# The MLP of the last two token blocks as seven half-size products per layer

## The chip, the cores and the metric

The kernel runs on one core of a Trainium2 chip. The metric is the device time in microseconds (us) of one execution. The engines are PE (TensorE, matrix products; PEld is its load of the stationary operand), DVE (VectorE), ACT (ScalarE), POOL (GpSimd) and SP (SyncE, which here issues the DMA transfers). SBUF holds the working tiles, PSUM the results of products in banks of 128 x 512 float32, and DRAM the inputs, outputs and scratch.

## The reference

One layer over 2048 tokens of 1024 channels, behind 16 learned meta tokens. A normed input is projected; two scans run over the sequence in chunks (a gated delta rule and a gated linear attention, four heads each); their gated outputs, 1024 columns wide, go through one output projection and are added to the input; then an MLP with squared ReLU, 1024 to 4096 to 1024, and a final norm.

```python
mix = jnp.concatenate([o_dn, o_gla], axis=-1).astype(x.dtype)
x = x + mix @ w_out
h2 = rmsnorm(x, norm2_g)
x = x + jnp.square(jax.nn.relu(h2 @ w_up)) @ w_down
...
return rmsnorm(h, final_norm_g)[:, CHUNK:]
```

The delta rule's state goes from chunk to chunk, so the mixed output of a block of tokens is complete only when the scan has passed its last chunk.

## The kernel before

The tokens are in four blocks of 512, the chunks in sixteen of 128, scanned in pairs. The program runs: input projection of blocks 0 and 1 (`phase_a`), scan of the meta tokens and of chunks 0 to 3, input projection of blocks 2 and 3, scan of chunks 4 to 11, `phase_c(0)`, scan of chunks 12 to 15, `phase_c(1)`, and `phase_c(2)` for blocks 2 and 3 together. `phase_c` is output projection and MLP. Most instructions of the program stand in the order that a scheduler gave them, so work of neighbouring calls is mixed: parts of the scan stand among the MLP's products, and block 1's output projection stands among the scan of chunk 11 to 13. Each engine runs its own list in order.

Channels lie on the partitions, tokens along the free dimension. Every product is made of three (L117 to L119): each float32 operand is split into a hi part, rounded to the PE's format, and a lo part, the difference, and hi x hi, lo x hi and hi x lo are summed in PSUM. A weight chunk of 128 x 1024 is loaded by SP into one of three raw buffers (L97), cast to hi by ACT (L101) and its lo part made by DVE (L102), in two buffers each. Activations are split the same way (L109 and L110; with a scale L112 and L113).

Per block the output projection has 192 products of 512 columns, the up layer 768 and the down layer 768. In `phase_c` the scan's output is read back from `mix_d` (L858), the projection is added to the input in `acc` (L896), `h2` is split from it, and the squares are summed in `tot` (ACT L882, POOL L883). The norm ahead of the MLP is made up for behind it (`norm`, L909 to L913), so the up layer starts without it. For each of eight groups g: four banks of the up layer, ReLU and square (L961, L962), split, and the group's share of the down layer, added to `acc` on DVE (L974). `finish` is the final norm: column sums of `tot` by PE (`pf`, L925), the power by POOL (L930), broadcast by PE (`pfb`, L939), eight scaled rows by DVE (L950) and the output. For block 0 and block 1 it is kept in `after` and run in the next scan pair or after `phase_c(1)`.

For blocks 2 and 3 each weight chunk serves both blocks, and the last of the eight groups goes by tokens, block 3 in two halves of 256, so that little is left after the last product.

The scan's mixed outputs are transposed (L812) and stored (L815) in `flush_mix`. A pair's triangular matrices are inverted on DVE in rows (L564, L570), and both U and the inverse V pass through DRAM (SP, L555, L560, L572, L578).

Of the kernel before, what the change touches and what calls it, by code (L numbers as in the profile page):

```python
# [8 lines left out]
F32 = mybir.dt.float32  # L9
# [7 lines left out]
D = 1024  # L17
SEQ = 2048
NMETA = 16
EPS = 1e-6  # L20
# [10 lines left out]
# log1p(e) = e * P(e) on [0, 1] to float32 accuracy.  # L31
# [10 lines left out]
def hybrid_kernel(ctx: ExitStack, tc: tile.TileContext, I: dict, out: bass.AP):  # L42
# [7 lines left out]
    wk = ctx.enter_context(tc.tile_pool(name="work", bufs=2))  # L50
# [70 lines left out]
    # ------------------------------------------------------------------ scratch in DRAM  # L121
# [6 lines left out]
    mix_d = [dp.tile([128, 8, TB], F32, name=f"mix_d{b}") for b in range(NB)]  # L128

    # ------------------------------------------------------------------ scan constants and state  # L130
# [21 lines left out]
    # ------------------------------------------------------------------ phase A: input projection  # L152
    def phase_a(b, kc, late=None):
# [3 lines left out]
        def log1p(e, p, shape, tag):  # L157
            """log(1 + e) for e in [0, 1], in a new tile."""
# [9 lines left out]
        def normless(k):  # L168
            """hi and lo parts of the transposed input times the norm gain, without 1 / rms."""
# [54 lines left out]
        def step(between):  # L224
            """the next part of each job; those that need a PSUM bank wait for the end of a group."""
# [84 lines left out]
        def gla_decay(sm, p, nt, dst, done=None):  # L310
            """cumulated log-sigmoid gates (before the division by the normalizer) into dst[j] of [128, nt * p]."""
# [29 lines left out]
        def gate_piece(y, t, c0, n):  # L341
            """columns c0..c0+n of the gates of token tile t: twice their silu."""
# [9 lines left out]
        def decays():  # L352
            """sets up the work on the decays; it runs in small parts among the groups."""
# [95 lines left out]
    # ------------------------------------------------------------------ phase B: the two scans  # L449
# [11 lines left out]
    def dn_pre(c):  # L461
        """everything of a chunk's delta rule that does not need the state; c None: the meta tokens."""
# [54 lines left out]
        # decay matrix, grams  # L517
# [24 lines left out]
    def dn_inverse(rs, vts):  # L542
        """V = (I - strict upper part of U)^-1 per chunk and head, into vts."""
# [44 lines left out]
            # 32 -> 64: the off-diagonal blocks of the two 64-blocks  # L588
# [21 lines left out]
            # 64 -> 128  # L610
# [10 lines left out]
    def post(po, scale, gate, mix):  # L621
        """per-head RMS norm of po * scale, times the gate."""
# [177 lines left out]
    after = []  # work on a block of tokens that is left for a later place  # L800
# [38 lines left out]

    # ------------------------------------------------------------------ phase C: output projection, MLP  # L840
    def phase_c(b0, pools, bank, kc, tail=None):
# [3 lines left out]
        nh = len(pools)  # L845
        # acc[i][k]: the residual stream of block i, channels 128 k..
        acc, xp = [], []
        for i, q in enumerate(pools):
            pairs = [k4("acc", q).rearrange("p (k t) -> p k t", k=2) for _ in range(4)]
            for j, t in enumerate(pairs):  # L850
                nc.sync.dma_start(out=t, in_=I["xT"][b0 + i, 2 * j : 2 * j + 2].rearrange("k p t -> p k t"))
            xp.append(pairs)
            acc.append([pairs[k // 2][:, k % 2, :] for k in range(NK)])
        mx = [[] for _ in pools]
        for i, q in enumerate(pools):
            for k in range(NK):
                m = tail.tile([128, 512], F32, name="mixk", tag="mixk", bufs=4) if tail else t512("mixk")
                nc.sync.dma_start(out=m, in_=mix_d[b0 + i][:, k, :])  # L858
                o = act("mx", q)
                split(m, *o, gain[:, k // 4 : k // 4 + 1])  # L860
                mx[i].append(o)

        def products(chunks, mov):
            """banks[j][i]: 128 output channels j of block i."""
            banks = [[bank("pc") for _ in pools] for _ in range(4)]
            last = len(chunks) - 1
            for c, src in enumerate(chunks):
                _, wh, wl = wchunk(src, 512)
                for j in range(4):
                    js = slice(j * 128, (j + 1) * 128)  # L870
# [264 lines left out]
```

## Time and profile before

| | us |
|---|---|
| median of three runs | 2658.26 |
| the runs | 2654.13 to 2667.26 |
| span of the profiled execution | 2658.3 |
| mean duration of a product of 128 x 512 in the MLP (they overlap) | 0.39 |
| lo part of a weight chunk, 128 x 1024, on DVE (mean) | 1.26 |
| hi part of a weight chunk on ACT (mean) | 1.05 |

The profile's page says for each engine how long it was busy. Its views list windows of time with busy times, the granted clock of PE and the DMA rate; groups of instructions by line; and the timeline, where a bracket behind a row gives the idle time of the engine before it and what ended that. L12 is line 12 of the kernel.

### The profile page before, as it was taken

What the parts mean: (1) busy time and instruction counts of PE and PEld (TensorE: products, weight loads), DVE (VectorE), ACT (ScalarE), POOL (GpSimd) and SP (SyncE); (2) the same over time, 40 slices, a digit from 0 to 9 for tenths busy, and PEclk for the clock granted to TensorE, in tenths of its full rate; (3) what the DMA queues carried; (4) which work ended last, traced back from release to release, by engine and by line L of the source; (5) the groups of instructions that cost most, each with busy time, mean ns of one, the idle gap of its engine ahead of it and who ended that gap; (6) DMA issues with size and microseconds to landing.
All of it is one profiled execution on the core that took longest, in us unless ns stands there. A gap on an engine that the chain in (4) does not pass through costs nothing.

```text
span 2658.3 us, 35430 instructions
## 1 busy us (share of the span) xinstructions
PE 2569.2 (97%) x13426; PEld 2127.1 (80%) x13426; DVE 1625.0 (61%) x3122; ACT 905.4 (34%) x1850; POOL 475.8 (18%) x385
## 2 busy tenths in 40 slices
PE   8999999999899999999998999999999999999998
PEld 6788688789678778888786888888888888888887
DVE  4777866985984875857679567555453343233335
ACT  4344345345334433334353243333321122112212
POOL 2123123223222321102044020101230000000003
PEclk9999999999999999999999999999999999999999
DMA  5264455355346323334363343253211111111111
GB/s 180 102 214 146 139 152 182 111 187 174 126 154 201 103 89 124 104 106 127 115 208 94 100 121 105 86 175 108 98 48 48 48 48 48 48 48 48 48 48 64
DMA packets 187122, 297.30 MB, mean 112 GB/s; under 512 B 33584, under 2 KB 116104, under 8 KB 186952
## 3 DMA queue, kind: packets, MB, share of 16 engines
q1 hardware_dynamic: 186952, 295.05, 35.5%
q8 instruction: 105, 1.72, 0.3%
q14 instruction: 65, 0.53, 0.1%
HBM read 244.62 MB, written 50.37 MB: 111 GB/s over the span
## 4 chain that ended last, share of the span: by engine, by line
PE 63%; DVE 9%; issue 2%; DMA 2%; POOL 1%; ACT 0%; SPq 0%; POOLq 0%; DVEq 0%; ACTq 0%
PE pc L119 18%; PE pc L118 18%; PE pc L117 18%; PE pa L117 2%; PE pa L118 2%; PE pa L119 2%; DVE wlo L102 1%; DVE inv_t L564 1%; DVE inv_v L570 1%; PE pks L650 1%; DVE l1p L163 0%; PE po L661 0%; PE pu L664 0%; PE po L660 0%; PE py L654 0%
## 5 line engine op out<-in xcount | busy, mean ns | idle before, releaser
L101 ACT CAST whi<-wraw 128x1024 fp32r<-128x1024 f32 (+1 forms) x344 | 346.9, 1009 | 1067.8 <-PE pc L118 813.0
L102 DVE TENSOR_TENSOR wlo<-wraw,whi 128x1024 fp32r<-128x1024 f32 (+1 forms) x280 | 344.8, 1232 | 576.3 <-ACT whi L101 575.2
L118 PE MATMUL pc<-avl,whi 128*128 128x512 f32 (+1 forms) x1056 | 413.1, 391 | 2.5 <-DVE avl L110 2.4
L117 PE MATMUL pc<-avh,whi 128*128 128x512 f32 (+1 forms) x1056 | 397.4, 392 | 12.2 <-DVE acc L974 12.0
L119 PE MATMUL pc<-avh,wlo 128*128 128x512 f32 (+1 forms) x1056 | 406.7, 389 | 0.0
L117 PE MATMUL pc<-h2h,whi 128*128 128x512 f32 x1024 | 402.0, 393 | 2.8 <-DVE acc L896 2.8
L118 PE MATMUL pc<-h2l,whi 128*128 128x512 f32 x1024 | 402.7, 393 | 0.0
L119 PE MATMUL pc<-h2h,wlo 128*128 128x512 f32 x1024 | 399.1, 396 | 1.1 <-DVE wlo L102 1.1
L117 PEld LDWEIGHTS pc<-avh,whi 128*128 128x128 f32 x1056 | 199.6, 189 | 57.3 <-issue 13.3
L118 PEld LDWEIGHTS pc<-avl,whi 128*128 128x128 f32 x1056 | 199.4, 189 | 47.1 <-DVE avl L110 4.8
L119 PEld LDWEIGHTS pc<-avh,wlo 128*128 128x128 f32 x1056 | 199.4, 189 | 42.8
L883 POOL TENSOR_TENSOR tot<-tot,sqk 128x512 f32<-128x512 f32 (+1 forms) x63 | 84.5, 1347 | 824.3 <-ACT sqk L882 822.5
L117 PEld LDWEIGHTS pc<-h2h,whi 128*128 128x128 f32 x1024 | 192.5, 188 | 46.1 <-DVE acc L896 4.1
L119 PEld LDWEIGHTS pc<-h2h,wlo 128*128 128x128 f32 x1024 | 192.3, 188 | 44.4 <-DVE wlo L102 1.9
L118 PEld LDWEIGHTS pc<-h2l,whi 128*128 128x128 f32 x1024 | 192.4, 188 | 42.6
L974 DVE TENSOR_TENSOR acc<-acc,pc 128x512 f32<-128x512 f32 x240 | 162.2, 685 | 104.3 <-PE pc L119 101.9
L102 POOL TENSOR_TENSOR wlo<-wraw,whi 128x780 fp32r<-128x780 f32 (+1 forms) x64 | 142.9, 2233 | 433.2 <-ACT whi L101 345.0
L117 PE MATMUL pa<-hh,whi 128*128 128x512 f32 x512 | 206.6, 405 | 4.2 <-ACT whi L101 2.3
L118 PE MATMUL pa<-hl,whi 128*128 128x512 f32 x512 | 202.7, 396 | 0.0
L119 PE MATMUL pa<-hh,wlo 128*128 128x512 f32 x512 | 188.8, 400 | 2.0 <-DVE wlo L102 1.2
L117 PE MATMUL pa<-whi,hh 128*128 128x390 f32 x512 | 167.8, 357 | 13.8 <-ACT hh L112 11.2
L118 PE MATMUL pa<-wlo,hh 128*128 128x390 f32 x512 | 180.4, 354 | 0.1
(274 smaller groups left out, 4079.7 us busy)
## 6 DMA issues: line engine op xcount, KB each, us to landing
wraw<-in_wup_dram SPq DMA_DIRECT2D x96, 512.0 KB, 3.6
wraw<-in_wdn_dram SPq DMA_DIRECT2D x96, 512.0 KB, 3.6
wraw<-in_wch_dram SPq DMA_DIRECT2D x64, 512.0 KB, 3.7
wraw<-in_wtk_dram SPq DMA_DIRECT2D x64, 390.0 KB, 3.9
qkv_d<-cy SPq DMA_DIRECT2D x48, 256.0 KB, 2.3
kqv<-qkv_d SPq DMA_DIRECT2D x16, 768.0 KB, 5.3
wraw<-in_wo_dram SPq DMA_DIRECT2D x24, 512.0 KB, 3.6
xk<-in_xT_dram SPq DMA_DIRECT2D x32, 256.0 KB, 4.2
```

The costliest lines, as they stand in the source:

```text
L101: A.copy(out=hi[:, :, 0:n], in_=raw[:, :, 0:n])
L102: eng.tensor_tensor(out=lo[:, :, 0:n], in0=raw[:, :, 0:n], in1=hi[:, :, 0:n].bitcast(F32), op=ALU.subtract)
L117: T.matmul(o, lhsT=ah, rhs=bh, start=first, stop=False)
L118: T.matmul(o, lhsT=ah, rhs=bl, start=False, stop=False)
L119: T.matmul(o, lhsT=al, rhs=bh, start=False, stop=last)
L564: V.tensor_tensor(out=t, in0=vv[:, 0:c, c : c + 1].broadcast_to([L, c, n]), in1=vv[:, c : c + 1, c + 1 : w].broadcast_to([L, c, n]), op=AL ...
L570: V.tensor_tensor(out=vv[:, 0:c, c + 1 : w], in0=vv[:, 0:c, c + 1 : w], in1=t, op=ALU.add)
L650: T.matmul(h4(pk)[:, h, :], lhsT=kg[:, h, :], rhs=S[:, h, :], start=True, stop=True)
L883: eng.tensor_tensor(out=tot, in0=tot, in1=sq, op=ALU.add)
L974: V.tensor_tensor(out=x, in0=x, in1=banks[j][i], op=ALU.add)
```

## The change

Blocks 0 and 1 are as before, one at a time. For blocks 2 and 3 the MLP's two layers are each taken as a product of 2 x 2 matrices of blocks, by Strassen's scheme in Winograd's form, with seven block products and not eight. The two columns of the moving operand are the two token blocks, its two rows the halves of the inner channels; the weights have two halves in each direction.

Four things follow in the program:

- **Own output projections.** `wo_block(2)` comes after the last scan pair in the program and ahead of `phase_c(1)`; `wo_block(3)` ahead of `phase_c(1)` too, with pools of its own and one buffer for its weights (`chunk1`). Each is normed ahead of the MLP (`token_scale`), stores its residual stream to `xs_d`, and block 2's normed rows go to `h2_d` in DRAM and come back.
- **The up layer.** Sums of the moving operand (B11, B21, T1 to T4, B22) are made once and split. Sixteen steps g follow, one for each 128 columns of both halves of the weights: the weight sums S1 to S4 on DVE, seven products of 12 matmuls, their combination on ACT, DVE and POOL, squared ReLU. The seven operands of the down layer are sums of the squares, and all are stored to `sq_d`.
- **The down layer.** Three passes of sixteen steps, two of the seven products in each (24 matmuls a step) in eight banks, the moving operands read back from `sq_d`; then the seventh product in two halves of 256 tokens.
- **The end.** The residual comes back from `xs_d`; block 2's final norm stands in the first half of the seventh product, those of block 3's halves behind their halves.

```diff
-    phase_c(0, [wk], mm, kc)
+    phase_c(0, kc)
     scan_pair(12)
     scan_pair(14)
-    phase_c(1, [wk], mm, kc)
+    x2 = [k4("acc") for _ in range(4)]
...
+    wo_block(2, kc, [act("mx") for _ in range(NK)], x2, tot2, mm, t512, None, *small2)
+    for k in range(NK):
+        nc.sync.dma_start(out=h2_d[:, k, :], in_=x2[k])
     run_after()
     scan.close()
-        phase_c(2, [wk2, wk], bank, kc, wk2)
+    last_pair(kc, wstack.close)
```

```diff
+    def wo_block(b, kc, mx, x, tot, bank, f512, chunk, dgt, rsp):
+        g2, fg, gain = kc
+        for k in range(NK):
+            nc.sync.dma_start(out=x[k], in_=I["xT"][b, k])
+            m = f512("mixk")
+            nc.sync.dma_start(out=m, in_=mix_d[b][:, k, :])
+            split(m, *mx[k], gain[:, k // 4 : k // 4 + 1])
+        for half in range(2):
+            banks = products([I["wo"][half, kk] for kk in range(4)], mx, bank, chunk)
+            for j in range(4):
+                k = 4 * half + j
+                V.tensor_tensor(out=x[k], in0=x[k], in1=banks[j], op=ALU.add)
+                nc.sync.dma_start(out=xs_d[b - 2][:, k, :], in_=x[k])
+                square_sum(tot, x[k], k == 0, f512)
+        rb = token_scale(tot, bank, dgt, rsp, EPS)
+        for k in range(NK):
+            V.scalar_tensor_tensor(out=x[k], in0=x[k], scalar=g2[:, k : k + 1], in1=rb, op0=ALU.mult, op1=ALU.mult)
```

```diff
+    def last_pair(kc, wk_close):
...
+        wo_block(3, kc, mx, x3, tot3, bank2, lambda name: r512(name, "x2", 8), chunk1, *small3)
+        x2 = [r512("x2", "x2", 8) for _ in range(NK)]
+        for k in range(NK):
+            nc.sync.dma_start(out=x2[k], in_=h2_d[:, k, :])
+        phase_c(1, kc)
+        run_after()
...
+        comb(t1, b12, b11)
+        comb(b12, b22, b12)
+        comb(b11, b12, b11, ALU.add)
+        comb(b21, b21, b11)
...
+        for name, src in (("T2", b11), ("T1", t1), ("T3", b12), ("B22", b22), ("T4", b21)):
+            ops[name] = operand_b(name)
+            for (hi, lo), x in zip(ops[name], src):
+                split(x, hi, lo)
...
+        for g in range(16):
...
+                V.tensor_tensor(out=s12[:, 0], in0=rc[:, 0], in1=rc[:, 1], op=ALU.add)
+                V.tensor_tensor(out=s12[:, 1], in0=s12[:, 0], in1=ra[:, 0], op=ALU.subtract)
...
+            def prod(a, b):
+                o = bank("p7")
+                for k in range(4):
+                    js = slice(k * 128, (k + 1) * 128)
+                    mm3(o, [x[:, js] for x in w[a]], ops[b][k], k == 0, k == 3)
+                return o
...
+            p = prod("A11", "B11")
+            A.copy(out=r1, in_=p)
+            p = prod("A12", "B21")
+            V.tensor_tensor(out=q11, in0=p, in1=r1, op=ALU.add)
+            p = prod("S2", "T2")
+            V.tensor_tensor(out=u, in0=p, in1=r1, op=ALU.add)
+            p = prod("S1", "T1")
+            A.copy(out=r5, in_=p)
+            G.tensor_tensor(out=q12, in0=u, in1=r5, op=ALU.add)
+            p = prod("S3", "T3")
+            V.tensor_tensor(out=u2, in0=p, in1=u, op=ALU.add)
+            G.tensor_tensor(out=q22, in0=u2, in1=r5, op=ALU.add)
+            p = prod("S4", "B22")
+            V.tensor_tensor(out=q12, in0=p, in1=q12, op=ALU.add)
+            p = prod("A22", "T4")
+            V.tensor_tensor(out=q21, in0=p, in1=u2, op=ALU.add)
...
+            V.tensor_tensor(out=c1, in0=q12, in1=q11, op=ALU.subtract)
...
+            for i, x in ((3, c1), (4, c3), (5, c2), (6, q21)):
+                nc.sync.dma_start(out=sq_d[i][:, g, :], in_=x)
...
+        for m in range(4):
+            with tc.high_priority(offset=HP):
+                V.tensor_tensor(out=r1[m], in0=r1[m], in1=bk[0][m], op=ALU.add)
+                u3 = e512("u3", "r", 4)
+                V.tensor_tensor(out=u3, in0=r1[m], in1=bk[1][m], op=ALU.add)
+            V.tensor_tensor(out=c21[m], in0=c21[m], in1=u3, op=ALU.add)
+            V.tensor_tensor(out=r1[m], in0=r1[m], in1=r5[m], op=ALU.add)
+            V.tensor_tensor(out=r5[m], in0=r5[m], in1=u3, op=ALU.add)
+        c12, c22 = r1, r5
+        residual(c12, 1, 0)
+        residual(c22, 1, 4)
...
+                        V.tensor_tensor(out=r[:, 0], in0=r[:, 0], in1=S[g], op=ALU.subtract)
...
+                    wpair(hi, lo, r[:, 0])
+                    S4.append((hi, lo))
+                b = moving((2,), g, cs)[0]
+                for m in range(4):
+                    js = slice(m * 128, (m + 1) * 128)
+                    mm3(bk[m][:, 0:256], [x[:, js] for x in S4[g]], b, g == 0, g == 15)
```

Three places in the order of the instructions show how the scheduler placed this.

The first is PE behind the last product of block 0's MLP. Before, after the intra-chunk products of chunk 11's linear attention (`pog`) and the first part of block 0's final norm (`pfb`), block 1's output projection (`mxh`, `mxl`) follows:

```order
L769 MATMUL pog<-gv,AT_124 128x128
L770 MATMUL pog<-Sg,gqg 128x128
L939 MATMUL pfb<-dg,ones 128x128
L117 MATMUL pc<-mxh,whi 128x512
L118 MATMUL pc<-mxl,whi 128x512
L119 MATMUL pc<-mxh,wlo 128x512
```

In the changed kernel the recurrence of chunk 11 (`pks`, `py`, `po`, `pu`), the transpose of its output (`pmix`) and the start of chunks 12 and 13 (`pk` to `pqk`) stand at this place, with no product of a projection between:

```order
L923 MATMUL pfb<-dg,ones 128x128 x2
L654 MATMUL pks<-S,kg 128x128 x4
L658 MATMUL py<-nkv,V_136 128x128 x4
...
L668 MATMUL pu<-vs,kdt 128x128 x4
L816 MATMUL pmix<-ident,mix 128x128 x4
L482 MATMUL pk<-ident,kqv 128x128 x4
...
L778 MATMUL pgu<-gv,gkdt 64x128 x4
...
L118 MATMUL pc<-mxh,whi 128x512 x4
```

The last row is the first product of block 2's projection, 147 matmuls behind the last one of the MLP. Its input `mixk` is loaded on SP behind the store of chunk 11's output, and this store behind four transfers of chunk 12's U:

```order
L819 DMA mix_d_97<-mixt 128x4x128
L831 DMA gate<-gate_d_85 128x512
L559 DMA inv_u_12971<-U 32x4x32 x4
L819 DMA mix_d_97<-mixt 128x4x128
L964 DMA mixk<-mix_d_97 128x512 x4
```

The second place is DVE at the end of block 1's MLP. Before, weights of the next projection (`wlo`) followed the final norm's eight scaled rows:

```order
L102 TENSOR_TENSOR wlo<-wraw,whi 128x1024
L929 TENSOR_SCALAR n_u<-pf 128x4
L936 TENSOR_SCALAR dg<-ident,n_r 128x128 x2
L950 SCALAR_TENSOR_TENSOR acc<-acc,fg,vb 128x512 x8
L102 TENSOR_TENSOR wlo<-wraw,whi 128x1024 x3
```

Now the lo parts of the operands T2, T1, T3, B22 and T4 stand behind these rows, and behind 17 of those the first lo part of a weight sum (`w7l` from the tile of S1 and S2), without which PE's third product can't go on:

```order
L926 SCALAR_TENSOR_TENSOR acc<-acc,fg,vb 128x512 x8
L1115 TENSOR_TENSOR s_17813<-w_17810 128x512
L1121 TENSOR_TENSOR s_17814<-w_17809,w_17810 128x512
L111 TENSOR_TENSOR T2l<-x_14910,T2h 128x512
L1116 TENSOR_TENSOR s_17813<-s_17813,w_17809 128x512
...
L111 TENSOR_TENSOR B22l<-x_14504,B22h 128x512
L111 TENSOR_TENSOR T4l<-x_14914,T4h 128x512
L1099 TENSOR_TENSOR w7l<-s_17813,w7h 128x1024
```

The third place is DVE in the first half of the seventh product of the down layer. The sums that take pass 3's banks (L1265, L1267) and combine them (L1268, L1269) stand between the sums that make S4 (L1326) and the lo parts of S4 (`s4l`) and of the squares (`bl`), on which PE's next products wait:

```order
L1326 TENSOR_TENSOR w_22594<-w_22594,sk 128x512
L1099 TENSOR_TENSOR s4l<-w_22569,s4h 128x512
L1267 TENSOR_TENSOR u_22312<-r_20928,p_21636 128x512
L1099 TENSOR_TENSOR bl<-br,bh 128x256
L1268 TENSOR_TENSOR c_21605<-c_21605,u_22294 128x512
L1269 TENSOR_TENSOR r_20925<-r_20925,r_21601 128x512
L1268 TENSOR_TENSOR c_21606<-c_21606,u_22300 128x512
```

Before there was no such place: each group's sums (L974) went into `acc` as the group ended.

More of the change, by code (lines that the diff above doesn't have):

```diff
@@ new lines, in square_sum, with products @@
+    def square_sum(tot, x, first, tmp, eng=G):
+        if first:
+            A.activation(out=tot, in_=x, func=AF.Square)
+            return
+        sq = tmp("sqk")[:, 0 : x.shape[-1]]
+        A.activation(out=sq, in_=x, func=AF.Square)
+        eng.tensor_tensor(out=tot, in0=tot, in1=sq, op=ALU.add)
+    def products(chunks, mov, bank, chunk=None):
+        banks = [bank("pc") for _ in range(4)]
+        last = len(chunks) - 1
+        for c, src in enumerate(chunks):
+            if chunk is None:
+                _, wh, wl = wchunk(src, 512)
+            else:
+                wh, wl = chunk(src)
+            for j in range(4):
+                js = slice(j * 128, (j + 1) * 128)
+                for k2 in range(2):
+                    w = (wh[:, k2, js], wl[:, k2, js])
+                    mm3(banks[j], w, mov[2 * c + k2], c == 0 and k2 == 0, c == last and k2 == 1)
+        return banks
@@ L915, in finish @@
-        def finish(i, c0, n, more=()):
-            cs = slice(c0, c0 + n)
-            nt = n // 128
-            terms = [tot[i][:, cs], *more]
-            pf = [bank("pf") for _ in range(nt if more else 1)]
+                x = acc[k]
+                V.tensor_tensor(out=x, in0=x, in1=banks[j], op=ALU.add)
+                o = act("h2")
+                split(x, *o, g2[:, k : k + 1])
+                h2.append(o)
+                square_sum(tot, x, k == 0, t512)
+        v = wk.tile([128, 512], F32, name="vb", tag="rb", bufs=1)
@@ L1004, in phase_c @@
-            with tc.high_priority(offset=HP):
-                for _ in late:
-                    pass
-        if tail is None:
-            after.append(lambda: [None for i in range(nh) for _ in finish(i, 0, TB)])
+            for half in range(2):
+                banks = products([I["wdn"][g, half, kk] for kk in range(2)], sq, mm)
+                for j in range(4):
+                    x = acc[4 * half + j]
+                    V.tensor_tensor(out=x, in0=x, in1=banks[j], op=ALU.add)
+                    if g == 7:
+                        square_sum(tot, x, False, t512)
```

451 lines of the change are left out of this document (316 added, 135 removed).

## The prediction

> **What bounds the kernel now.** I read the page's busy shares and its chain of work first, then the windows by stage, then single stretches of the timeline.
>
> ```profile
> span 2658.3 us, 35430 instructions
> PE 2569.2 (97%) x13426; PEld 2127.1 (80%) x13426; DVE 1625.0 (61%) x3122; ACT 905.4 (34%) x1850; POOL 475.8 (18%) x385
> PE 63%; DVE 9%; issue 2%; DMA 2%; POOL 1%; ACT 0%; SPq 0%; POOLq 0%; DVEq 0%; ACTq 0%
> ```
>
> PE is busy in 97% of the span and is most of the chain that ended last; no other engine is near it. So time goes down by what PE is spared, and up by every place where PE has nothing to run. The stages, from the windows (columns: length, then busy time and count of PE, PEld, DVE, ACT and POOL, granted clock, DMA share, GB/s):
>
> ```profile
> 1345.70:1836.00 490.30, 479.08 (x2608) 393.40 (x2607) 331.33 (x636) 187.54 (x408) 87.50 (x76) 0.99 0.41 127
> 1836.00:2645.10 809.10, 807.89 (x3592) 658.56 (x3590) 304.85 (x401) 178.19 (x261) 70.14 (x55) 1.00 0.17 53
> 2645.10:2658.30 13.20, 2.28 (x12) 1.90 (x12) 6.43 (x18) 1.43 (x4) 0.71 (x1) 0.69 0.40 140
> 2400.00:2500.00 100.00, 100.00 (x433) 81.07 (x432) 33.70 (x44) 20.16 (x29) 0.00 (x0) 1.00 0.15 47
> 2620.00:2630.00 10.00, 10.00 (x88) 10.00 (x87) 2.96 (x9) 2.79 (x7) 5.76 (x7) 1.00 0.01 2
> ```
>
> The first row is the scan of chunks 12 to 15 with block 1; the second is blocks 2 and 3; the third is what is left after the last product. The fourth gives the pace of a product of 512 columns: 100 / 433 = 0.231 us (records last 0.39, but overlap). The fifth gives 10 / 88 = 0.114 us for 256 columns; I take 0.118, the step between the last ones of the kernel. A block has 192 products for its projection and 768 for each layer of its MLP; in block 3 the last 96 go as 192 of half width. So blocks 2 and 3 are 3360 x 0.231 + 192 x 0.118 = 799 of their 809 us.
>
> **What is removed.** Up to the end of block 0's MLP (1345.7) the order of PE and DVE doesn't change, so 1345.7 stays. In the second stage the two output projections of blocks 2 and 3 come in, 2 x 192 products: 490.3 + 384 x 0.231 = 579.0. The third stage becomes 16 steps of 84 and 48 of 24 products of 512 columns, 2496, and twice 16 x 12 of 256: 2496 x 0.231 + 384 x 0.118 = 576.6 + 45.3 = 621.9. With the tail of 13.2: 1345.7 + 579.0 + 621.9 + 13.2 = **2559.8**, that is 98.5 us less, 88.7 of it (384 x 0.231) for the eighth product that Strassen's scheme saves in each layer. Everything below is given back.
>
> **Joint a: block 0's MLP to block 2's output projection.** Before, block 1's projection stood there, whose input was long stored. Now it is block 2's, whose last part comes from chunk 11, still in the scan.
>
> ```profile
> 1345.48 0.40 PE L119 MATMUL pc<-avh,wlo 128*128 128x512 f32 x1
> 1345.71 0.38 PE L661 MATMUL po<-vs,at 128*128 128x128 f32 x2
> 1345.93 0.39 PE L660 MATMUL po<-S,qg 128*128 128x128 f32 x2
> 1355.54 0.48 PE L117 MATMUL pc<-mxh,whi 128*128 128x512 f32 x1
> 1364.90 6.98 DVE L950 SCALAR_TENSOR_TENSOR acc<-acc,fg,vb 128x512 f32<-128x512 f32 x8 [0.89 <-ACT vb L944]
> 1388.17 1.12 DVE L634 SCALAR_TENSOR_TENSOR mix<-po,f_r,gate 128x128 f32<-128x128 f32 x4
> mix_d<-mixt SPq DMA_DIRECT2D x32, 256.0 KB, 2.6
> mixk<-mix_d SPq DMA_DIRECT2D x32, 256.0 KB, 4.0
> ```
>
> Before, PE went on with a projection 9.8 us after the last product. The chain through chunk 11 ended with its mix at 1389.3, mixed with projection work on PE and DVE; without that, and still behind the eight rows of block 0's final scaling (6.98), I estimate 1380. Then come the transpose, its place on SP behind four transfers of chunk 12's U, the store (2.6), the load (4.0) and one split: the first product of block 2 stands near 1392, 46 us after the last. In between PE has 147 scan products, mostly 128x128 at 0.22 us (1345.71 to 1345.93): about 29 us. Loss 17 us, between 8 (the chain shrinks further) and 24.
>
> **Joint b: block 2's to block 1's projection.** PE has only parts of chunk 12's solve, which need the inverse through DRAM, and the block's norm.
>
> ```profile
> 1467.73 0.18 DVE L570 TENSOR_TENSOR inv_v<-inv_v,inv_t 32x30 f32<-32x30 f32 x1
> 1475.60 0.70 DVE L586 STREAM_TRANSPOSE wt<-V 128x512 f32<-128x512 f32 x1
> 1835.08 0.69 DVE L974 TENSOR_TENSOR acc<-acc,pc 128x512 f32<-128x512 f32 x1 [0.20 <-PE pc L119]
> 1853.13 5.39 DVE L950 SCALAR_TENSOR_TENSOR acc<-acc,fg,vb 128x512 f32<-128x512 f32 x8 [5.46 <-ACT vb L944]
> ```
>
> From the inverse's last row to the transpose were 7.7 us; the order puts that last row beside the projection's last sums. With the solve's first products, their copies and the norm's, block 1's first product starts some 12 us late; after its first 24 the second chunk's lo part is late by 5 more, behind the eight scaled rows (5.39). Loss 17; bounds 8 and 24, the latter being the way from the last sum to the end of the scaling in the last two rows (23.4).
>
> **The clock behind a stall** is a cost of its own:
>
> ```profile
> 1450.00:1460.00 10.00, 5.04 (x21) 3.47 (x19) 9.93 (x8) 1.85 (x2) 10.00 (x7) 0.94 0.01 3
> 1460.00:1470.00 10.00, 8.23 (x28) 6.67 (x29) 7.49 (x21) 0.00 (x0) 0.24 (x2) 0.72 0.40 117
> 1461.77 0.76 PE L117 MATMUL pc<-avh,whi 128*128 128x512 f32 x1 [5.85 <-DVE acc L974]
> ```
>
> PE waited 5.85 us for DVE, and the next 10 us had a granted clock of 0.72: 2.8 us lost after the wait. I add 3 us at each of joints a and b (a has scan work within it, so the two together get 3), c and e.
>
> The Trainium skill ("TensorE: Matmul & The Clock Gate", "What's actually happening") says that the clock falls to half after one idle window of about 3.4 us and that 3.4 us of work raise it again, which speaks against this change, since each new joint would pay twice. By its figures a restart would lose 1.7 us, an estimate, where the window above lost 2.8; the sum would be about 4 us lower.
>
> **Joint c: block 1's MLP to the up layer.** DVE does the final scaling of block 1 first, as in the last pair of rows above but with less on PE in its way, so I estimate it to end 17 us after the last sum. Behind it stand, by the order, three sums of weights, 17 splits of operands and the lo part of S1 and S2:
>
> ```profile
> L110 DVE TENSOR_TENSOR avl<-rl,avh 128x512 fp32r<-128x512 f32 x128 | 92.4, 723 | 1.9 <-ACT avh L109 0.7
> L102 DVE TENSOR_TENSOR wlo<-wraw,whi 128x1024 fp32r<-128x1024 f32 x248 | 313.2, 1263 | 514.2 <-ACT whi L101 513.2
> ```
>
> 21 rows at 0.6 to 0.72 are 12.6 to 15, and 1.26: ready after 31 us. PE has the 24 products on B11 and B21, eight on hi parts and the norm's: 9 us. Loss 22; bounds 14 and 32 (the way of 18.05 before scaling in block 1 of before, kept whole).
>
> **Up layer.** A step of 84 products is 84 x 0.231 = 19.4 us. Beside it:
>
> ```profile
> L974 DVE TENSOR_TENSOR acc<-acc,pc 128x512 f32<-128x512 f32 x240 | 162.2, 685 | 104.3 <-PE pc L119 101.9
> L883 POOL TENSOR_TENSOR tot<-tot,sqk 128x512 f32<-128x512 f32 x52 | 76.3, 1474 | 818.0 <-ACT sqk L882 816.3
> L101 ACT CAST whi<-wraw 128x1024 fp32r<-128x1024 f32 x280 | 293.3, 1048 | 958.0 <-PE pc L118 813.0 <-PE pa L118 60.5 <-issue 36.2
> 1860.00:1870.00 10.00, 10.00 (x44) 8.08 (x43) 1.14 (x1) 0.01 (x1) 0.00 (x0) 1.00 1.04 389
> ```
>
> DVE has 13 rows of 0.69, a half lo part (0.7) and three whole ones (3.8): 13.4 us. ACT: three casts of 1.05, one of 0.6 and ten passes of 0.6, 9.8 us. POOL: two sums of 1.47. DMA moves 1 MB of weights and 1.75 MB of squares, 2.75 MB in 19.4 us = 142 GB/s, where 389 were reached. PE covers all; cost 0, with what it would be if DVE were late among the rivals. The change to the down layer waits once for squares just stored: 3 us (0 to 6).
>
> **Down layer.** A step of 24 products is 5.5 us, beside it 1 MB of DMA (182 GB/s), two lo parts on DVE and at most two sums (4.0 us): hidden. The seventh product's first half is not: PE needs 192 x 0.118 = 22.7 us, while DVE has 28 sums from pass 3 (28 x 0.69 = 19.3) between some 11 sums and 12 lo parts of S4 (15) and the squares' lo parts (5): 39 us. Loss 16, plus 3 at the second half, where DVE waits for a norm before further lo parts; bounds 10 and 30. **Block 3's projection** (one weight buffer) runs inside block 1's MLP, 24 and 21 products in turn: 4 us (0 to 9). The tail has the same steps: 0, perhaps 1 less.
>
> **Sum:** a 17, b 17, their clock 3, c 22 + 3, d 3, down 19 + 3, block 3 4, tail -1: 90. 2559.8 + 90 = **2650 us**, 8 below the profiled execution, whose span of 2658.3 equals the runs' median of 2658.26.
>
> **Rivals.** *The joints cost half* (45): the scheduler's waits overlap more than I see, since my estimates are chains of rows in one queue and before had only short stalls in the same stretches (PE busy 479 of 490). 2559.8 + 45 = 2605. Against it: the order of DVE at c and in the down layer is fixed, and its sums are plain.
>
> *Slower: the ring of weight operands in the up layer.* Two buffers hold A1, S12, S34 in turn. S34's buffer comes free when PE has done its second product, 5.5 us into a step; hi (1.05) and lo (1.26) follow at 8, and PE asks for S34 at product 5, 11.1 us. From 3.1 us of lateness it decides every step. POOL's sums can make DVE late:
>
> ```profile
> 1445.70 14.39 POOL L911 TENSOR_TENSOR acc<-acc,vb 128x512 f32<-128x512 f32 x8 [16.23 <-DVE vb L909]
> 1450.60 1.45 DVE L564 TENSOR_TENSOR inv_t<-inv_v 32x210 f32<-32x210 f32 x1
> 1460.33 0.34 DVE L570 TENSOR_TENSOR inv_v<-inv_v,inv_t 32x184 f32<-32x184 f32 x1
> ```
>
> While POOL summed, a small DVE row took 1.45 us, behind it 0.34. Two such sums a step can push S34's lo part back by 2.9, and evacuations that DVE has in front of it (0.69 each) by three more: 5.2, 2.1 too late, 16 x 2.1 = 33: 2683. Against it: DVE is idle 6 of the 19.4 us. The Trainium skill ("SBUF — State Buffer", "SBUF: two separate sides") calls that shared port an exclusive lock held for a whole instruction, so that the loser blocks; these rows agree.
>
> *The scheme doesn't save what it says:* the order has 384 products of 512 columns fewer in sum; excluded.
>
> **How the numbers follow.** Forecast 0.60, half the joints 0.18, the ring 0.17, rest 0.05. The joints' half widths (8, 8, 9, 10, 4.5, 3) add in squares to 18: the forecast alone is 2632 to 2668. The range reaches over both rivals, 2600 to 2688. A measurement can tell 0.5% of this kernel, 13 us: below 2645 lie a third of the forecast and the first rival, 0.40; within, most of the forecast, 0.35; above 2671.5 the ring, a little of the forecast and the rest, 0.25.
>
> **What would show it.** In the changed profile: PE's idle time at the four joints by its releaser (a: DMA of mixk, b: DVE wt and wlo, c: DVE w7l, down: DVE s4l), 17, 17, 22 and 16; up-layer steps of 19.4 (the ring: over 21); down steps of 5.5. Wrong it would be if a down step shows DMA waits, or if the stretch from block 1's end to the tail is not near 622 + 50.

## The result, and the profile after

The changed kernel took 2679.68 us (median, 2675.24 to 2682.84), the kernel before 2658.11 beside it: ratio 1.0079, 95% interval 1.0057 to 1.0101. It is 21 us slower, where 8 us faster was forecast; the time lies inside the range.

The page of the changed kernel: span, busy share and count by engine, and the chain that ended last by engine.

```profile
span 2681.0 us, 36393 instructions
PE 2532.2 (94%) x13166; PEld 2088.1 (78%) x13166; DVE 1823.8 (68%) x3415; ACT 1057.6 (39%) x2099; POOL 497.6 (19%) x398
PE 58%; DVE 11%; DMA 6%; issue 2%; ACT 1%; POOL 1%; SPq 0%; DVEq 0%; POOLq 0%; ACTq 0%
```

PE is busy 37 us less than before (2569.2), yet the span grew by 22.7: the time outside PE grew by 60. In the chain DMA rose from 2% to 6% and DVE from 9% to 11%. The same by stages, from the windows (columns as before):

```profile
0.00:1355.50 1355.50, 1296.95 (x7216) 1080.01 (x7217) 987.50 (x2069) 538.74 (x1179) 320.94 (x255) 0.98 0.45 140
1355.50:1977.70 622.20, 588.54 (x3020) 477.64 (x3019) 390.56 (x718) 220.91 (x460) 101.88 (x91) 0.97 0.40 130
1977.70:2314.20 336.50, 318.10 (x1361) 257.66 (x1359) 217.59 (x298) 161.37 (x250) 54.53 (x36) 0.96 0.44 148
2314.20:2593.00 278.80, 266.82 (x1153) 214.80 (x1152) 161.53 (x207) 106.61 (x145) 0.00 (x0) 1.00 0.56 186
2593.00:2666.90 73.90, 58.73 (x408) 55.29 (x408) 60.79 (x108) 27.79 (x63) 19.61 (x16) 0.88 0.48 156
2666.90:2681.00 14.10, 3.08 (x13) 2.71 (x12) 5.81 (x17) 2.16 (x6) 0.69 (x1) 0.54 0.26 84
```

Against the terms of the prediction (its stalls put into their stages), in us:

| stage | forecast | measured | difference |
|---|---|---|---|
| up to the end of block 0's MLP | 1345.7 | 1355.5 | +9.8 |
| scan, block 2's projection, block 1, block 3's projection | 579.0 + 41 = 620.0 | 622.2 | +2.2 |
| up layer, with joint c | 310.5 + 25 = 335.5 | 336.5 | +1.0 |
| down layer, three passes, with d | 266.1 + 3 = 269.1 | 278.8 | +9.7 |
| seventh product | 45.3 + 22 = 67.3 | 73.9 | +6.6 |
| tail | 12.2 | 14.1 | +1.9 |

Three stages make 26 of the 31 us of the miss (2681.0 against 2650): the first, in which nothing was thought to change, the down layer, which was thought hidden, and the seventh product. Each is read more closely.

**The first stage.** Its windows have the same count of instructions on every engine before and after, and in the same order. Before, it was:

```profile
0.00:1345.70 1345.70, 1279.94 (x7216) 1073.25 (x7217) 982.37 (x2069) 538.22 (x1179) 317.47 (x255) 0.98 0.45 141
```

PE is busy 17 us more for the same 7216 products, at the same granted clock of 0.98. No single wait appears; the lag grows as products go by: PE began block 0's projection (`mxh`) at 848.9 before and at 854.7 now, and ended block 0's MLP at 1345.5 and at 1355.3. The groups of instructions by line say what is longer: each product is. Columns: total busy, mean ns of one. Before, then after:

```profile
L118 PE MATMUL pc<-h2l,whi 128*128 128x512 f32 x1024 | 402.7, 393 | 0.0
L118 PE MATMUL pa<-hl,whi 128*128 128x512 f32 x512 | 202.7, 396 | 0.0
```

```profile
L119 PE MATMUL pa<-hl,whi 128*128 128x512 f32 x512 | 207.1, 405 | 0.0
L119 PE MATMUL pc<-h2l,whi 128*128 128x512 f32 x512 | 203.6, 398 | 0.0
```

5 to 9 ns more for a product of the same shape from the same tiles, with no wait ahead of any. What the diff changes for these products is where a tile lies: three small constants went from the pool `work` into `const`, which is allocated first, so the weight buffers moved up by 96 bytes (29888 to 29984 in each partition) and the activations stayed (63168).

**Pass 3 of the down layer** has DVE waiting for DMA. The timeline of DVE (start, length, what it waited for), and SP's queue beside it:

```profile
2540.38 0.69 DVE L1257 TENSOR_TENSOR sk<-sk,w 128x512 f32<-128x512 f32 x1 [3.12 <-DMA w<-in_dn_dram]
2540.98 0.68 DVE L1258 TENSOR_TENSOR w<-w 128x512 f32<-128x512 f32 x1
2541.59 0.68 DVE L1099 TENSOR_TENSOR w7l<-sk,w7h 128x512 fp32r<-128x512 f32 x1
2542.19 0.68 DVE L1099 TENSOR_TENSOR w7l<-w,w7h 128x512 fp32r<-128x512 f32 x1
2542.79 1.22 DVE L1099 TENSOR_TENSOR bl<-br,bh 128x1024 fp32r<-128x1024 f32 x1
2546.95 0.69 DVE L1257 TENSOR_TENSOR sk<-sk,w 128x512 f32<-128x512 f32 x1 [2.94 <-DMA w<-in_dn_dram]
```

```profile
2536.15 0.55 SPq L1207 DMA_DIRECT2D w<-in_dn_dram  x1
2542.90 0.55 SPq L1207 DMA_DIRECT2D w<-in_dn_dram  x1
```

A step takes 2546.95 - 2540.38 = 6.6 us where PE needs 24 x 0.231 = 5.5. The load of a weight is issued (2542.90) when the lo part that ends at 2542.87 frees one of three raw buffers. In DVE's list the sum for that very load (L1257, in front by its high priority) stands two rows on, so DVE stands still until it has landed, some 4 us after its issue, and only then makes the lo parts that free the next buffer. The waits of DVE in this pass and of PE from 2490 to 2592.5 (total, times, longest), and the window of the pass, which takes 96.1 us where 384 x 0.231 are 88.7:

```profile
DVE sk L1257 <- DMA w<-in_dn_dram: 29.2, 12, 3.6
PE p L120 <- DVE w7l L1099: 6.8, 10, 1.4
```

```profile
2495.90:2592.00 96.10, 88.88 (x377) 70.01 (x378) 61.58 (x89) 31.40 (x47) 0.00 (x0) 1.00 0.47 156
```

**The seventh product** waits for DVE's list, as forecast, and pays three times in clock. PE's waits in 2592.5 to 2667 (waits under 1.2 us in total left out), and PE's timeline around the last clock loss:

```profile
PE p L119 <- DVE bl L1099: 7.7, 6, 2.1
PE p L120 <- DVE s4l L1099: 3.2, 2, 2.7
PE p L118 <- DVE r L1265: 2.9, 2, 2.0
```

```profile
2627.78 0.64 PE L119 MATMUL p<-bl,s4h 128*128 128x256 f32 x4
2631.13 1.23 PE L120 MATMUL p<-bh,s4l 128*128 128x256 f32 x4 [2.70 <-DVE s4l L1099]
2632.15 0.41 PE L118 MATMUL p<-bh,s4h 128*128 128x256 f32 x1
2632.36 0.41 PE L119 MATMUL p<-bl,s4h 128*128 128x256 f32 x1
2638.50 0.28 PE L120 MATMUL p<-bh,s4l 128*128 128x256 f32 x1
2638.61 0.28 PE L118 MATMUL p<-bh,s4h 128*128 128x256 f32 x1
```

Behind the wait of 2.70 products of 256 columns follow each other in 0.21 us (2632.15 to 2632.36), and from 2638.5 on in 0.12 again, as before the wait. Two earlier waits, of 2.01 us (ended at 2596.30) and 1.94 us (ended at 2602.63), were followed by the same within 1 us. The granted clock (third figure from the right) in the windows 2596 to 2600, 2600 to 2610 and 2630 to 2640:

```profile
2596.00:2600.00 4.00, 3.70 (x18) 3.71 (x19) 4.00 (x8) 1.03 (x3) 0.00 (x0) 0.57 0.24 80
2600.00:2610.00 10.00, 5.99 (x31) 5.49 (x31) 10.00 (x19) 2.35 (x5) 0.00 (x0) 0.66 0.27 87
2630.00:2640.00 10.00, 8.17 (x43) 7.70 (x44) 8.90 (x12) 4.84 (x11) 7.75 (x6) 0.66 0.14 42
```

The lo part of S4 that ends the wait of 2.70 is one of four consecutive rows of DVE that took 1.75 to 1.78 us, where such a row takes 0.69 before (2614.07): POOL summed squares for a norm beside them. This lengthening of DVE's list was not in the forecast's sum, and no run takes these sums off POOL.

The joints came near the forecast. Joints a, b and c on PE's timeline (first product of block 2's projection, the two waits of joint b, first product of block 1's, and the two long waits of the up layer):

```profile
1401.44 1.86 PE L118 MATMUL pc<-mxh,whi 128*128 128x512 f32 x4 [2.72 <-ACT mxh L113]
1452.83 1.81 PE L986 MATMUL pf<-ones,tot 128*128 128x1 f32 x8 [4.61 <-POOL tot L851]
1456.56 0.63 PE L598 MATMUL pr<-wt,U 32*32 32x32 f32 x16 [1.92 <-DVE wt L590]
1459.67 0.77 PE L118 MATMUL pc<-mxh,whi 128*128 128x512 f32 x1
2001.29 0.79 PE L118 MATMUL p<-T2h,w7h 128*128 128x512 f32 x1 [10.45 <-ACT w7h L1098]
2010.72 0.80 PE L120 MATMUL p<-T2h,w7l 128*128 128x512 f32 x1 [2.75 <-DVE w7l L1099]
```

### The profile page after: what moved, and what is told of

It reads as the page before. It is cut to its first block, busy times and chain, and to the rows that moved or that the text cites. A ratio compares the mean times of both kernels' runs of the same rounds, so it can differ in the third digit from the quotient of the medians.

```text
span 2681.0 us, 36393 instructions
## 1 busy us (share of the span) xinstructions
PE 2532.2 (94%) x13166; PEld 2088.1 (78%) x13166; DVE 1823.8 (68%) x3415; ACT 1057.6 (39%) x2099; POOL 497.6 (19%) x398
## 4 chain that ended last, share of the span: by engine, by line
PE 58%; DVE 11%; DMA 6%; issue 2%; ACT 1%; POOL 1%; SPq 0%; DVEq 0%; POOLq 0%; ACTq 0%
PE pc L118 10%; PE pc L120 10%; PE pc L119 10%; PE p L120 6%; PE p L118 6%; PE p L119 6%; DMA w<-in_dn_dram 3%; PE pa L118 2%; PE pa L119 2%; PE pa L120 2%; DVE w7l L1099 1%; DVE wlo L103 1%; DVE inv_v L574 1%; DVE inv_t L568 1%; DMA mixk<-mix_d 1%
## 5 line engine op out<-in xcount | busy, mean ns | idle before, releaser
L118 PE MATMUL pc<-avh,whi 128*128 128x512 f32 x512 | 194.5, 407 | 16.1 <-DVE acc L947 6.3
L119 PE MATMUL pc<-avl,whi 128*128 128x512 f32 x512 | 206.1, 402 | 0.3 <-DVE avl L111 0.2
L118 PE MATMUL pc<-h2h,whi 128*128 128x512 f32 x512 | 203.9, 398 | 1.7 <-DVE acc L895 1.7
L119 PE MATMUL pc<-h2l,whi 128*128 128x512 f32 x512 | 203.6, 398 | 0.0
L120 PE MATMUL pc<-avh,wlo 128*128 128x512 f32 x512 | 201.3, 400 | 0.0
L120 PE MATMUL pc<-h2h,wlo 128*128 128x512 f32 x512 | 199.5, 400 | 0.7 <-DVE wlo L103 0.7
L120 PE MATMUL pa<-whi,hl 128*128 128x390 f32 x512 | 174.2, 349 | 0.2 <-DVE hl L114 0.2
L120 PE MATMUL p<-bh,w7l 128*128 128x512 f32 x384 | 144.7, 394 | 8.5 <-DVE w7l L1099 8.3
L118 PE MATMUL p<-bh,w7h 128*128 128x512 f32 x384 | 147.5, 390 | 2.9 <-ACT bh L1098 1.4
L119 PE MATMUL p<-bl,w7h 128*128 128x512 f32 x384 | 149.5, 389 | 0.0
```

Source lines behind the costliest of these rows:

```text
L118: T.matmul(o, lhsT=ah, rhs=bh, start=first, stop=False)
L119: T.matmul(o, lhsT=ah, rhs=bl, start=False, stop=False)
L120: T.matmul(o, lhsT=al, rhs=bh, start=False, stop=last)
```

## The experiments

All times are medians beside runs of the kernel before on the same chip; ratios are to it, with their 95% intervals. The changed kernel has 1.0079.

**1 and 2. Addresses alone.** The theory: the pace of a product hangs on where its two operands lie relative to each other. First, the kernel before, with only the place of the three constants taken from the change; no instruction and no order is different:

```diff
-    g2 = small("g2", [128, NK])
-    gain = small("gain", [128, 2])
-    fg = small("fg", [128, NK])
+    g2 = const("g2", [128, NK])
+    gain = const("gain", [128, 2])
+    fg = const("fg", [128, NK])
```

> The kernel before, with the three small tiles g2, gain and fg in the constants' pool, as the change has them; the order of every engine stays as it was, only the weight tiles whi and wlo lie 96 bytes further on. Theory (pace of PE hangs on whether its two SBUF operands lie at the same place of a 128-byte line): in the traces of before and after a product takes 0.229 us where the two addresses agree modulo 128 and 0.231 to 0.233 where they don't; with the shift 5168 products of 512 columns and 1536 of 390 lose that agreement and some 700 gain it, worked out +21.6 us: about 2680, and +10 of it by the end of block 0's MLP. Rival (the first 1345 us of the changed kernel were 9.8 us longer by run-to-run variation, or by something else of the change): 2658, no difference beyond 0.3%.

Measured: 2674.22 us, ratio 1.0054 (1.0039 to 1.0069), 15 us slower: about two thirds of what was expected. A kernel whose instructions stand in the same order on every engine became slower by moving a buffer 96 bytes. The last product of block 0's MLP began at 1354.43, 8.9 us later than in the kernel before (1345.48), where +10 was expected, and the product of the input projection that took 396 ns takes 403:

```profile
L118 PE MATMUL pa<-hl,whi 128*128 128x512 f32 x512 | 206.4, 403 | 0.0
```

Then the other way, the changed kernel with an unused tile of 96 bytes, which puts activations and weights back into their old relation:

```diff
+    small("pad", [128, 24])
     g1 = small("g1", [128, NK], I["g1"])
```

> The changed kernel with 96 unused bytes at the start of the work pool, so that its tiles lie as the weights do again, modulo 128; order unchanged. Address theory: 3648 products of 512 and 1536 of 390 columns win the agreement back, worked out -20 us: about 2660, block 0's MLP ends near 1346. Rival (no such effect): 2680.

Measured: 2663.11 us, ratio 1.0018 (1.0008 to 1.0027): 17 us of the loss are gone, and block 0's MLP ended at 1340.7, earlier than the 1346 expected. The group by line of this run shows the product back at its old length (398 ns without the tile):

```profile
L119 PE MATMUL pc<-h2l,whi 128*128 128x512 f32 x512 | 200.5, 392 | 0.0
```

**3. The rule behind it**, in a kernel of its own, run once: eight stages of 192 products of 128 x 512 on the same two inputs, in which only the places of the operands differ; the reference isn't computed. Modulo 256 bytes, moving operand minus stationary operand is 128, 32, 192, 96, 96, 0, 160 and 64 in the eight stages.

> Nothing of the reference is computed: eight stages of 192 products of 512 columns on the same two operands, whose places in SBUF alone differ: stationary at 0 modulo 128 in the first four stages and at 32 in the last four, moving at 0, 32, 64, 96 in each four. Address theory: 0.227 to 0.229 us a product in stage 1 and stage 6, where the two agree, 0.231 to 0.234 in the others. Rival (a slow place is one of the moving operand alone, or of neither): stages 5 to 8 as 1 to 4, or all alike.

The copies that end the stages, on ACT's timeline:

```profile
52.59 0.59 ACT L77 COPY o<-p 128x512 f32<-128x512 f32 x1 [45.57 <-PE p L75]
97.38 0.59 ACT L77 COPY o<-p 128x512 f32<-128x512 f32 x1 [44.20 <-PE p L75]
142.22 0.59 ACT L77 COPY o<-p 128x512 f32<-128x512 f32 x1 [44.25 <-PE p L75]
187.01 0.59 ACT L77 COPY o<-p 128x512 f32<-128x512 f32 x1 [44.21 <-PE p L75]
231.81 0.59 ACT L77 COPY o<-p 128x512 f32<-128x512 f32 x1 [44.21 <-PE p L75]
275.37 0.59 ACT L77 COPY o<-p 128x512 f32<-128x512 f32 x1 [42.97 <-PE p L75]
320.35 0.59 ACT L77 COPY o<-p 128x512 f32<-128x512 f32 x1 [44.39 <-PE p L75]
365.14 0.59 ACT L77 COPY o<-p 128x512 f32<-128x512 f32 x1 [44.21 <-PE p L75]
```

From copy to copy 44.8 to 45.0 us in every stage but the sixth, the one with a difference of 0: 275.37 - 231.81 = 43.56. That is 0.2333 against 0.2269 us a product, 2.8%. A difference of 128 is no better than any other (the first stage, read by its count of products in equal windows, is as slow as the second). So the rule as expected, modulo 128, failed in the first stage, and that it is modulo 256 is read off one stage of this run. Matched with the addresses in the compiled program, the kernel before bears it out: 4457 products with a difference of 0 are followed by the next after 0.229 us on average, 355 with 128 after 0.231. It holds for long runs of such products; in experiment 1 the 351 with a difference of 0, which stand among others, take 0.232.

**4. The same in the kernel before:** the tiles `av` of the down layer are 2080 bytes apart and so stand at every residue. With a distance of 2112 and two paddings, 6704 and not 4788 of the 8352 products of 512 columns have operands that agree modulo 256, by the addresses in the compiled program.

```diff
-        return q.tile([128, TB + 4], dt, name=name, tag="av", bufs=8)
+        if not avpad:
+            avpad.append(wk.tile([128, 8], F32, name="avpad", bufs=1))
+        return q.tile([128, TB + 16 if q is wk else TB], dt, name=name, tag="av", bufs=8)
...
+        wk2.tile([128, 16], F32, name="pad2", bufs=1)
```

> The kernel before with padding alone (the av tiles 2112 bytes apart in the work pool, the second work pool shifted): same order on every engine. Address theory: products whose operands agree modulo 128 go from 5160 to 7256 of 8352; by the paces of the trace -9.7 us, and by what b_shift and a_pad showed of such sums (0.7 and 0.85 of them) -7 to -8: about 2651. Rival (only a disagreement of whole stages counts): 2659.

Measured: 2646.0 us, ratio 0.9951 (0.9935 to 0.9966): 12 us faster, somewhat more than expected, with no instruction moved.

**5. Joints a and b:** block 2's projection moved behind the scan, into `last_pair` ahead of block 3's, with its single weight buffer. Block 1's projection then follows block 0's MLP as before the change.

```diff
-    wo_block(2, kc, [act("mx") for _ in range(NK)], x2, tot2, mm, t512, None, *small2)
...
+        wo_block(2, kc, operand(opa, "mx") + operand(opa, "mx"), x2, r512("tot3", "tot3", 1), bank2, lambda name: r512(name, "x3", 8), chunk1, *small3)
```

> The changed kernel with block 2's output projection moved behind the scan, beside that of block 3 and with its single weight buffer, so that block 1's projection can again follow block 0's MLP. Theory (joints a and b cost about 17 each and 3 of clock, since block 2's input is late and block 1's is not): -25 to -37, of which 4 to 9 come back as the second projection with one weight buffer beside block 1's MLP: 2648 to 2660. Rival (PE's stalls there are the scan's own and come back elsewhere): 2675 to 2685.

Measured: 2653.08 us, ratio 0.9976 (0.9966 to 0.9986), 27 us less than the change. The first product after block 0's MLP is back early, at 1364.72, behind a last product at 1354.45 in this run; it was 46 us behind in the changed kernel:

```profile
1364.72 0.48 PE L118 MATMUL pc<-mxh,whi 128*128 128x512 f32 x1
```

**6. Pass 3:** its two sums (L1257, L1258) on POOL, which has nothing else there, so that DVE's list no longer waits for the load.

> The changed kernel with the two weight sums of pass 3 of the down layer on POOL, which is idle there, and not on DVE. Theory (DVE runs its list in order, and the sum of the step three ahead stands in it right behind the lo parts that free its buffer, so DVE waits out a load of 4 us in each step: load, two sums, two lo parts, 6.5 us, more than PE's 5.4): pass 3 goes from 97 us to about 87, and the time to 2668 to 2672. Rival (the loads themselves, 1 MB a step in pieces of 2 KB, are the limit): pass 3 stays at 97, 2680.

Measured: 2667.93 us, ratio 1.0031 (1.0019 to 1.0042), 12 us less. The three passes take 261.8 us from their first to their last product, where the change has 276.2; the rival is refuted. The last window of the down layer in this run has PE without a gap:

```profile
2490.00:2572.60 82.60, 82.59 (x365) 68.03 (x363) 58.81 (x58) 31.94 (x48) 39.39 (x25) 1.00 0.52 173
```

**7. The seventh product:** as 6, and the sum for S4 (L1326) on POOL as well.

> As a_pool3 (weight sums of pass 3 on POOL), and the sixteen sums that make S4 for the seventh product on POOL too. Theory (the first half of the seventh product waits for DVE, which has some 39 us of rows there against PE's 22.7): DVE has 16 x 0.6 = 9.6 us less, the seventh product's two halves go from 74 us to 64 to 68, the time to 2658 to 2663. Rival (PE waits there for loads or for POOL's own sums of 1.3 us): as a_pool3, 2668.

Measured: 2661.82 us, ratio 1.0016 (1.0006 to 1.0025). The time is in the expected range, but not by the expected way: from its first to its last product the seventh took 72.8 us in 6 and 73.5 here, and the intervals of 6 and 7 meet. A gain at this place is not shown. PE waits there no less in all, now for the lo parts of the squares:

```profile
PE p L119 <- DVE bl L1099: 16.4, 9, 3.9
```

DVE has fewer rows here, but beside POOL's sums, of 1.71 us each, some are longer: the lo part of S4 takes 1096 ns on average in this stretch, where it takes 783 in 6. How much of the gain that took isn't separated.

**8. All repairs together** (2, 5, 6 and 7):

> The changed kernel with a_pad, a_wo2 and a_pool7 together. If the costs are of different places they add: 2680 - 17 - 27 - 12 - 7 = 2617, under the kernel before by 42. If block 2's projection beside block 1's MLP or POOL's sums collide with each other's cover: 2625 to 2640.

Measured: 2624.6 us, ratio 0.9873 (0.985 to 0.9896): faster than both kernels, 33 us below the one before.

**9. And all remaining addresses:** four paddings, after which all products of 256 and more columns in the program but 42 have operands that agree modulo 256.

```diff
-        return q.tile([128, TB + 4], dt, name=name, tag="av", bufs=8)
+        if not avpad:
+            avpad.append(wk.tile([128, 56], F32, name="avpad", bufs=1))
+        return q.tile([128, TB + 64], dt, name=name, tag="av", bufs=8)
...
+        pad_p = ctx.enter_context(tc.tile_pool(name="padp", bufs=1, side="right"))
+        pad_p.tile([128, 48], F32, name="opad", bufs=1)
...
+        raw_s.enter_context(tc.tile_pool(name="padr", bufs=1, side="right")).tile([128, 48], F32, name="rpad", bufs=1)
```

> The version with the three repairs (a_sum, 2624.6 us), order of every engine unchanged; four paddings of 192 to 256 bytes put the remaining 2304 products of 512 columns and 192 of 256 on operands whose addresses agree modulo 256. Theory (the pace follows that agreement): the microbenchmark gave 0.2333 - 0.2269 = 0.0064 us a product, the traces of before and after some 0.004 on average for the residues concerned; where PE is the bound, 2400 x 0.004 to 0.0064 = 10 to 15 us less: 2610 to 2615. Rival (the gain of a_pad and b_av came from where tiles lie in other respects, the one residue that was moved there): no change, 2622 to 2627.

Measured: 2617.35 us, ratio 0.9854 (0.9832 to 0.9875). 7 us less, about half of what was expected, and the intervals of 8 and 9 meet: it agrees with the theory in sign only. It is the fastest of all that ran, 41 us below the kernel before beside it and 29 below the kernel before with experiment 4's paddings.

**10. What the seventh product waits for:** as 9, with S4 of steps 0 to 7 made beside the last eight steps of pass 3.

```diff
         for g in range(16):
+            if g >= 8:
+                s4(g - 8)
             r = wraw(g, slice(0, 4, 2))
```

> The repaired and aligned version (a_best, 2617.35 us; its stretch of the seventh product 2524.5 to 2599.3 = 74.8 us) with the operand S4 of steps 0 to 7 (load, difference, split) made beside the last eight steps of pass 3, where VectorE now has room, and not beside the seventh product. Theory (the seventh product waits for VectorE's list, where the lo parts of S4 and of the squares stand among pass 3's sums): some 8 lo parts of 0.69 = 5.5 us leave that list, and with less waiting the clock falls less: the stretch is 5 to 10 us shorter, 2607 to 2612. Rival (it waits for the sums of pass 3 themselves and for the lo parts of the squares behind them, which stay in the list): 0 to 2 us, 2615 to 2618.

Measured: 2620.57 us, ratio 0.9855 (0.9839 to 0.9872): no gain. The stretch of the seventh product did become shorter, 66.8 us (2536.0 to 2602.8) against 74.8, as the theory had it. But the three passes took 269.5 us from their first to their last product, where 9 has 262.3, and the seventh product began 3.2 us after their last: DVE now waits in pass 3 for the hi parts of S4 on ACT (total, times, longest), and the gain is given back.

```profile
DVE s4l L1110 <- ACT s4h L1109: 23.8, 10, 4.3
```

## Why the prediction was wrong

The size of the scheme itself was right: 384 products of 512 columns are gone, and PE's busy time fell. What the joints take came near the forecast too. The side was missed by two steps that put a cost at nothing, and a third that was too small.

- **"The order of PE and DVE doesn't change, so 1345.7 stays"** failed. The order did stay; the addresses didn't. The pace of 0.231 was read in one stage and carried to all products as if it belonged to the shape. Experiments 1 and 2 put the 96 bytes at 15 and 17 us, from both sides, and 3 shows the rule. In the profiled execution 9.8 of it stand in the first stage and about 4 in the second (622.2 us from the last product of block 0's MLP to the last of block 1's, 618.3 with the padding of experiment 2). The split is rough: in experiments 5, 6 and 7, whose first stage has the same order and addresses as the change, that stage ended at 1354.5, 1350.3 and 1347.8, so that single profiles of it scatter by 7 us; the cost itself rests on the medians of 1 and 2.
- **"Down layer: … hidden"** failed in pass 3, by what the prediction had named as the sign ("if a down step shows DMA waits"). The sum over DVE's work (4.0 of 5.5 us) was right; a list in order that holds a wait for a load which its own later rows release isn't covered by idle time. 9.7 us in the windows of the three passes, 7.4 of it in pass 3 (96.1 against 88.7); 12 by experiment 6.
- **"Loss 16, plus 3"** at the seventh product had the right mechanism, DVE's list, and was too small: 28.6 against 22. The waits on PE named above come to 7.7 + 3.2 + 2.9 = 13.8; the granted clock in the three windows above (0.57 over 4 us, 0.66 over 10 twice) is at most 1.7 + 6.8 = 8.5 more, where one drop of 3 was counted. Experiment 10 fits the list (8 us shorter once half of S4 is made ahead, though its loads, POOL's sums and ACT's hi parts went along), and 7 shows that taking the sums for S4 off DVE gains nothing when they go to POOL. How the rest of the 28.6 is divided, and how much of it is POOL's hold on DVE, stays open.
- **Joint a** held: first product 46 us behind the last, as forecast (1355.27 to 1401.44). **Joint b** held in its first part, 12 us late; the 5 us more that were counted behind the first 24 products did not come (from 1459 to 1500 PE has no wait above 0.3 us). **Joint c** held in size: 336.5 - 310.5 = 26 against 25. The way was in part another. PE's 10.45 us ended with the hi part of S1 and S2 on ACT, which stands there behind 17 hi parts of operands; DVE had made their sums, behind block 1's final scaling, 0.9 us before. Of the two long waits only the 2.75 us ended with DVE's `w7l`, as forecast. No run moves this joint, so its cause is read, not tested. Experiment 5 took back 27 us of a and b, for which 37 were counted with the clock.
- **The rivals.** Half the joints: refuted by the same rows. The ring of weight operands: refuted, since behind joint c the up layer shows no lateness (PE has no wait from 2015 to 2314, and a step takes 19.28 us, from 2044.49 to 2063.77). The rival on the slower side was priced near the measured time (2683) for a reason that didn't occur.

Without the two steps that were put at nothing the forecast stands: 2663.11 with the padding, less the 12 of experiment 6, is 2651, an estimate, where 2650 was said. Some of that closeness is luck: the 6.6 us of the seventh product are still in it, against them the 5 of joint b that did not come.

## What to carry to other kernels

Before a stage is taken over as unchanged, compare not only the order of its instructions but the addresses of its operands: a constant moved to another pool can cost as much as a joint (15 to 17 us here). Where a sum over an engine's work says "hidden", look in that engine's list for a wait on a load whose buffer is freed by rows behind that wait; a cheap mend is an engine that has nothing else there, as long as its work doesn't lengthen the rows of the first. And a scheme that saves an eighth of PE's products in two layers gives it back at every place where PE has to wait for something made just in time; repaired together with the 96 bytes, these were worth 55 us here (2679.68 to 2624.6).

## What the runs showed of the hardware

A product of 128 x 512 follows the last in 0.2269 us when the addresses of its stationary and its moving operand in SBUF agree modulo 256 bytes, and in 0.2333 to 0.2343 when they don't; differences of 32, 64, 96, 128, 160 and 192 are alike within that (experiment 3, one stage for the first and seven for the second). Which part of the memory makes that so isn't shown. In whole kernels it was worth +15, -17 and -12 us (experiments 1, 2 and 4).

In the seventh product the granted clock fell three times, with waits of PE of only 2.01, 1.94 and 2.70 us among shorter ones (means of 0.57, 0.66 and 0.66 in the windows shown), and products then ran at 0.21 where 0.12 is their pace, for some 3 to 7 us. The Trainium skill ("TensorE: Matmul & The Clock Gate", "What's actually happening") speaks of an idle window of about 3.4 us; these waits are shorter and the clock fell all the same, so the measurement decides here.

While POOL summed squares beside the seventh product (7.75 us busy in the window from 2630), single rows of DVE that take 0.69 us elsewhere took 1.75 there. Moving sums to POOL can cost that where DVE is the bound; the longer rows of experiment 7 point the same way:

```profile
2629.32 1.75 DVE L1099 TENSOR_TENSOR s4l<-w,s4h 128x512 fp32r<-128x512 f32 x1
2630.99 1.76 DVE L1326 TENSOR_TENSOR w<-w,sk 128x512 f32<-128x512 f32 x1
```
